# A two-layer hybrid decoder trunk on one core: v and probabilities copied by ScalarE, and another split of the first phase's side work

## The chip, the cores and the metric

The kernel runs on one core of one Trainium2 chip. The metric is the device time of one execution in microseconds. Engine names in the rows: PE is TensorE, PEld its weight loads, DVE is VectorE, ACT is ScalarE, POOL is GpSimd, SP is the engine that issues the DMAs.

## The reference

512 tokens of width 1024 go through two layers; each layer is a feed-forward half step, a token mixer and a second feed-forward half step, all in float32. Cut to what matters:

```python
for l in range(2):
    mod = (silu(c) @ w_ada[l] + b_ada[l]).reshape(b, 9, d)
    h = rmsnorm(x, norm_g[l, 0]) * (1 + mod[:, 1]) + mod[:, 0]
    x = x + 0.5 * mod[:, 2] * swiglu(h, w_ffn_in[l, 0], w_ffn_out[l, 0])
    h = rmsnorm(x, norm_g[l, 1]) * (1 + mod[:, 4]) + mod[:, 3]
    x = x + mod[:, 5] * token_mixer(h, l, ...)
    h = rmsnorm(x, norm_g[l, 2]) * (1 + mod[:, 7]) + mod[:, 6]
    x = x + 0.5 * mod[:, 8] * swiglu(h, w_ffn_in[l, 1], w_ffn_out[l, 1])

def token_mixer(h):                       # three branches, gated and summed
    qa, ka, va, qb, kb, vb, u = split(h @ w_in)
    # A: 8 heads of 64, three dilated windows, combined by their denominators
    # B: 4 heads, difference of two softmaxes: p0 / sum(p0) - lam * p1 / sum(p1)
    # C: GLU, causal depthwise convolution of 31 taps, layer norm, swish
    y = sum_i sigmoid(h @ w_gate_i) * (branch_i @ w_branch_i)
    return y @ w_out
```

## The kernel before

**Products.** Activations lie with the 1024 features on partitions, as 8 chunks of 128 x 512 tokens. Each float32 operand is held as a high and a low half, and each product is three TensorE matmuls: high by high, high by low, low by high (`mm_steps`; the rows show them as L274, L276 and L278). For a weight tile, `halves` makes the high half `wh` by a ScalarE copy (L226) and the low half `wl` by a subtraction (L230), on VectorE mostly, and on GpSimd for the weights of the first phase (`kind == "first"`) and a few others (`second`). Weights come by DMA on SP's queue into 5 raw tiles; `load` issues the DMA and the two halves, and `weight` keeps two weights loaded ahead (`AHEAD`) before it hands one out.

**Six stages.** Feed-forward 1 takes the time to about 355 us, mixer 1 to 956, the other two feed-forwards of the middle to 1644, mixer 2 to 2217 and the last feed-forward the rest. In feed-forward 1 the first phase works on the fly: for each chunk k, `first(k)` normalizes chunk k (`norm_h`: `hx` on VectorE, L491; `hh`, its high half, on ScalarE, L493; `hl`, its low half, on VectorE, L500), and TensorE then does 18 products of 512 columns with chunk k and the weight `("first", k)` into six PSUM banks. Between `hx` and `hl` stands `modulation(k + 1)`: it makes the modulation vectors of the next chunk. `ada` (L430, L431) loads a 128 x 1024 weight and multiplies and sums it with the broadcast `cb`; `ada_done` adds the bias and makes the 128x1 columns `amp` (L444, L445) and `shift` (L442), all on VectorE. After the phase stand a plain block (m = 3) and pairs of blocks by Strassen-like products (`pair`, L583), whose seven weights come in the order p = 1, 2, 6, 7, 5, 3, 4 from four raw tiles (`block`, L242 to L254). `more(k)` between the blocks puts k further `ada` jobs, the modulation vectors that later stages need, behind each.

**Attention.** In the mixer, `project` makes q, k and v of a pair of A heads or of one B head: PSUM to `qk` by ScalarE (L841), to the high half of v by VectorE (L842) and to its low half by VectorE (L843). `scores` does six products of 64 rows (three for each half of the partitions, L896) into two PSUM banks of the tag `s`, VectorE adds the bias and takes the maximum (L903, `m`), ScalarE the exponential (L905), VectorE the reciprocal of the denominator (L921). `sa` then scales the probabilities by it on VectorE: both halves in an A head (L925), one of them in a B head (L928). `sb` transposes the probabilities on TensorE (L938) into a bank of `s` and splits them into halves (`pT`, L268 and L269); `pv` and `sc` multiply them with v (L965, L980, L983). These steps of one head and the projection of the next are woven into each other by generators (`pull`), and the convolution's taps (L770, VectorE, 240 in all) are put among them by a rhythm.

**What sets the order.** A tile scheduler lays down each engine's static order from its own estimates; semaphores then make an engine wait at run time. In `setup` and `first`, `manual_schedule` keeps VectorE in program order. PSUM has 4 banks of the tag `mm`, 3 of `s` and 1 of `o`; `whi` and `wlo` have 3 tiles each.

Of the kernel before, what the change touches and what calls it, by code (L numbers as in the profile page):

```python
# [16 lines left out]
AF = mybir.ActivationFunctionType  # L17
# [5 lines left out]
D = 1024  # L23
# [50 lines left out]
class Trunk:  # L74
# [146 lines left out]
    def halves(self, key, raw, n):  # L221
        nc = self.nc
        kind = key[0]
        hi = self.wp.tile([P, 1024], F32R, tag="whi", name=self.name("wh"), bufs=3)
        lo = self.wp.tile([P, 1024], F32R, tag="wlo", name=self.name("wl"), bufs=3)
        nc.scalar.activation(hi[:, :n], raw[:, :n], AF.Copy)  # L226

        second = (kind == "u" and key[2] == 0) or (kind == "in" and key[3:] == (0, 1))
        eng = nc.gpsimd if kind == "first" or second else nc.vector
        eng.tensor_tensor(lo[:, :n], raw[:, :n], hi[:, :n].bitcast(F32), op=ALU.subtract)  # L230
        return hi, lo

# [102 lines left out]
    def setup(self):  # L335
        nc, io, cp = self.nc, self.io, self.cp
        self.par = cp.tile([P, L, NPAR], F32, name="par")
        row = self.t4k([P, D], F32, "crow")
        nc.scalar.dma_start(row[0:1, :], io["c"])
        nc.scalar.dma_start(self.par[:, 0, :], io["par"][:, 0, :])  # L340
        xt = cp.tile([P, KD, T], F32, name="x")
        self.x = [xt[:, k, :] for k in range(KD)]
        for k in range(0, KD, 2):
            nc.sync.dma_start(xt[:, k:k + 2, :], io["x"][:, k:k + 2, :])
        self.h = [(cp.tile([P, T], F32R, name=f"hh{k}"), cp.tile([P, T], F32R, name=f"hl{k}"))
                  for k in range(KD)]
        self.acc = cp.tile([P, T], F32, name="ssq")
        self.sq7 = cp.tile([P, T], F32, name="sq7")
        self.ident = cp.tile([P, P], F32, name="ident")
        make_identity(nc, self.ident)  # L350
        self.ones = cp.tile([P, 2], F32, name="ones")
        nc.vector.memset(self.ones, 1.0)
        self.mod = [cp.tile([P, 72], F32, name=f"mod{l}") for l in range(L)]
        self.shift = [cp.tile([P, 24], F32, name=f"shift{l}") for l in range(L)]
        self.amp = [cp.tile([P, 24], F32, name=f"amp{l}") for l in range(L)]
        self.res = [cp.tile([P, 24], F32, name=f"res{l}") for l in range(L)]
        nc.scalar.activation(row[0:1, :], row[0:1, :], AF.Silu)
        cb = self.t4k([P, D], F32, "cb")
        for a in range(0, D, T):
            ps = self.bank("mm")  # L360
            nc.tensor.matmul(ps, self.ones[0:1, 0:1].to_broadcast([1, P]), row[0:1, a:a + T],
                             start=True, stop=True)
            nc.scalar.activation(cb[:, a:a + T], ps, AF.Copy)
        for k in range(KD):
            sq = self.t2k("sq") if k > 1 else (self.acc, self.sq7)[k]
            nc.scalar.activation(sq, self.x[k], AF.Square)
            if k > 1:
                a = (self.acc, self.sq7)[k % 2]
                nc.vector.tensor_tensor(a, a, sq, op=ALU.add)
        nc.vector.tensor_tensor(self.acc, self.acc, self.sq7, op=ALU.add)  # L370
        self.ada(cb, 0, 8)
        v = self.token_sum([self.acc], range(4), 1.0 / D, EPS)
        return cb, self.token_bcast(self.rsqrt(v, 4), range(4))

    def p(self, l, o, n=1):
        return self.par[:, l, o:o + n]
# [269 lines left out]
    def ffn(self, n, l, f, ada, cb, stats, nxt, first=None):  # L646
        nc, io = self.nc, self.io
        s = 2 * f
        acts = {}

        def finish(m, pg, pu):
            sl = self.t2k("sil")
            nc.scalar.activation(sl, pg, AF.Silu)
            nc.vector.tensor_tensor(sl, sl, pu, op=ALU.mult)
            acts[m] = self.act_pair("a")
            self.split(acts[m], sl)

        def unit(g):
            return lambda d: self.weight("down", l, f, g, d)

        def more(k):
            for _ in range(k):
                if ada:
                    ada.popleft()(cb)

        if first:
            banks = [self.bank(t) for t in ("mm", "mm", "mm", "mm", "s", "s")]
            for k in range(KD):
                w = first(k)
                for j in range(6):  # L670
                    self.mm(banks[j], w, slice(j * P, (j + 1) * P), self.h[k], k == 0, k == KD - 1)
            for m in range(3):
                finish(m, banks[2 * m], banks[2 * m + 1])
            self.sums()
            self.ready = True
        early = []
        blocks = self.ffn_blocks(n)
        st = {}
        for (kind, i), after in zip(blocks, blocks[1:] + [("end", 0)]):
            if kind == "plain":  # L680
                if i == 0:
                    early = self.head(lambda j: self.weight("in", l, f, j // 2, j % 2))
                    self.sums()
                ps = []
                for j in range(2):
                    if early:
                        ps.append(early.pop(0))
                        continue
                    w = self.weight("in", l, f, i, j)
                    ps.append(self.bank("mm"))  # L690
                    self.mmk(ps[j], w, self.h, range(KD), 0, KD - 1)
                finish(i, ps[0], ps[1])
                if first:
                    more(4)
            elif kind == "pair":
                down = (lambda g=after[1]: self.down(l, f, g, 0, acts)) if after[0] == "down" else None
                st = self.pair(l, f, i, st, after[1] if after[0] == "pair" else None, acts, down)
                if first or i > 2:
                    more(2 if first else 1)
            else:  # L700
                more(2)
                for d in range(1, KD):
                    self.down(l, f, i, d, acts)
                    more(2)
        more(len(ada or ()))
        self.tail(l, s, unit(2), acts, GROUPS[2], GROUPS[2][0], stats, nxt)
# [110 lines left out]
    def project(self, l, i, st):  # L817
# [3 lines left out]
        for sub in range(4):  # L821
# [4 lines left out]
            for t in range(4):  # L826
                for kk in range(2):
                    k = sub * 2 + kk
                    hs = slice(t * P, (t + 1) * P)
                    ws = slice(kk * 384, (kk + 1) * 384)  # L830
                    hi, lo = self.h[k]
                    o = ps[t][:, 0:384]
                    nc.tensor.matmul(o, hi[:, hs], w[0][:, ws], start=k == 0, stop=False)  # L833
                    yield
                    nc.tensor.matmul(o, hi[:, hs], w[1][:, ws], start=False, stop=False)  # L835
                    yield
                    nc.tensor.matmul(o, lo[:, hs], w[0][:, ws], start=False, stop=k == KD - 1)  # L837
                    if k < KD - 1:
                        yield
                if sub == 3:  # L840
                    nc.scalar.activation(qk[:, t, :], ps[t][:, 0:256], AF.Copy)  # L841
                    nc.vector.tensor_copy(v[:, 0, t, :], ps[t][:, 256:384])  # L842
                    nc.vector.tensor_tensor(v[:, 1, t, :], ps[t][:, 256:384],  # L843
                                            v[:, 0, t, :].bitcast(F32), op=ALU.subtract)
                    if t == 3:
                        self.qk_norm(l, i, st)
                    yield
# [61 lines left out]
    def attention(self, l, i, st, ys, pull, before):  # L909
# [6 lines left out]
        def sa(n):  # L916
# [5 lines left out]
            if A:  # L922
                dat[n] = [e0, e1]
                for j, e in enumerate(dat[n]):
                    nc.vector.tensor_scalar(e[:, 0:w], e[:, 0:w], rd[:, j:j + 1], None, op0=ALU.mult)  # L925
                return
            nc.vector.tensor_tensor(rd[:, 1:2], rd[:, 1:2], self.neglam[:, l:l + 1], op=ALU.mult)
            nc.vector.tensor_scalar(e1[:, 0:w], e1[:, 0:w], rd[:, 1:2], None, op0=ALU.mult)  # L928
            nc.vector.scalar_tensor_tensor(e0[:, 0:w], e0[:, 0:w], rd[:, 0:1], e1[:, 0:w],
                                           op0=ALU.mult, op1=ALU.add)  # L930
            dat[n] = [e0]
# [196 lines left out]
    def run(self, stop=6):  # L1128
        nc, io = self.nc, self.io

        def modulation(k):
            if k < KD:
                if k:
                    self.ada(cb, 0, 8 + k)
                self.ada(cb, 0, k)
                self.ada_done(0, 0, 1, (k, k + 1))
                self.ada_done(0, 0, 0, (k, k + 1))

        def first(k):
            with self.tc.manual_schedule(engines={mybir.EngineType.DVE}):  # L1140
                self.norm_h(0, 0, k, pb, FULL, lambda: modulation(k + 1))
            return self.weight("first", k)

        with self.tc.manual_schedule(engines={mybir.EngineType.DVE}):
            cb, pb = self.setup()
# [100 lines left out]
```

## Time and profile before

| | us |
|---|---|
| Median of 3 runs | 2555.83 (2554.1 to 2555.9) |
| The profiled execution | 2555.3 |
| Its span in the profile | 2553.2 |
| PE busy | 2486.7 (97%) |
| DVE busy | 1965.9 (77%) |
| ACT busy | 1123.4 (44%) |
| POOL busy | 30.6 (1%) |
| Mean granted clock of TensorE | 0.992 |

The span counts from the first to the last recorded instruction; 2.1 us of the execution lie outside of it. TensorE's clock has two levels, and 1.00 in the rows is 2.4 GHz. A matmul's busy time overlaps with that of the next, so the distance between two starts tells more than the duration. Rows of the timeline put several like instructions into one (x2, x6); an entry in brackets is the idle time ahead of it and what ended it.

### The profile page before, as it was taken

The page shows a single profiled execution, that of the slowest core. Times are in us where ns is not written, and L with a number is a line of the kernel's source. Part 1 is how long each engine was busy: PE and PEld are TensorE (multiplying, and loading weights), DVE is VectorE, ACT ScalarE, POOL GpSimd, SP SyncE. Part 2 cuts the span into 40 slices and gives each one's busy share as a digit, 9 for nine tenths or more (in the row PEclk, how much of TensorE's full clock was granted, in tenths as well). Part 3 has the DMA queues.
Part 4 walks back from the last instruction along what each step waited for, and adds up shares of the span by engine and source line. Part 5 has one row for each costly group of instructions (what it writes and reads, how often), then busy time and mean ns, then how long its engine had stood idle before and what let it go on. Part 6 is the DMA issues. An engine that isn't in the chain of part 4 may idle for free.

```text
span 2553.2 us, 37958 instructions
## 1 busy us (share of the span) xinstructions
PE 2486.7 (97%) x15072; PEld 2192.3 (86%) x15072; DVE 1965.9 (77%) x3519; ACT 1123.4 (44%) x1765; POOL 30.6 (1%) x33
## 2 busy tenths in 40 slices
PE   6899999999999999999989999999999999999999
PEld 5889898888778889898989898888787788898988
DVE  8998876999965478979678886679999554885855
ACT  4435343554553355343455252435555433552523
POOL 2000000000000000000000000000000000000000
PEclk9999999999999999999999999999999999999999
DMA  7564744312223323737324554332122233233332
GB/s 268 165 248 149 247 146 127 91 57 75 79 83 108 91 75 101 263 101 263 108 67 143 213 167 148 99 87 75 54 84 75 75 115 91 65 103 99 109 97 85
DMA packets 97747, 312.20 MB, mean 122 GB/s; under 512 B 10345, under 2 KB 17257, under 8 KB 97570
## 3 DMA queue, kind: packets, MB, share of 16 engines
q1 hardware_dynamic: 97424, 309.65, 38.1%
q8 instruction: 118, 1.93, 0.3%
q14 instruction: 59, 0.48, 0.1%
q10 hardware_dynamic: 146, 0.14, 0.0%
HBM read 307.62 MB, written 6.06 MB: 123 GB/s over the span
## 4 chain that ended last, share of the span: by engine, by line
PE 81%; DVE 12%; ACT 3%; DMA 2%; issue 2%; POOL 0%; DVEq 0%; SPq 0%; ACTq 0%
PE mm L583 15%; PE mm L274 14%; PE mm L276 14%; PE mm L278 14%; PE s L583 11%; PE mm L837 3%; PE mm L835 3%; PE mm L833 3%; DVE wl L230 2%; PE s L896 2%; DVE wr L770 1%; DMA wr<-in_w_up 1%; PE o L965 1%; PE s L938 1%; DVE ada L431 1%
## 5 line engine op out<-in xcount | busy, mean ns | idle before, releaser
L226 ACT ACTIVATE wh<-wr 128x1024 fp32r<-128x1024 f32 (+1 forms) x481 | 485.3, 1010 | 623.8 <-PE mm L278 299.0
L230 DVE TENSOR_TENSOR wl<-wr,wh 128x1024 fp32r<-128x1024 f32 (+1 forms) x468 | 544.3, 1165 | 206.3 <-ACT wh L226 205.1
L274 PE MATMUL mm<-ah,wh 128*128 128x512 f32 (+1 forms) x752 | 287.2, 383 | 0.0
L278 PE MATMUL mm<-al,wh 128*128 128x512 f32 (+1 forms) x752 | 286.7, 382 | 0.0
L276 PE MATMUL mm<-hh,wl 128*128 128x512 f32 (+1 forms) x776 | 281.5, 366 | 5.2 <-DVE wl L230 5.2
L276 PE MATMUL mm<-ah,wl 128*128 128x512 f32 (+1 forms) x752 | 286.3, 382 | 0.0
L274 PE MATMUL mm<-hh,wh 128*128 128x512 f32 (+1 forms) x776 | 281.5, 366 | 5.0 <-ACT hh L493 2.7
L583 PE MATMUL mm<-sh,wh 128*128 128x256 f32 x936 | 268.8, 287 | 16.9 <-ACT wh L226 14.1
L278 PE MATMUL mm<-hl,wh 128*128 128x512 f32 (+1 forms) x776 | 276.2, 367 | 5.8 <-DVE hl L500 5.6
L583 PE MATMUL mm<-sh,wl 128*128 128x256 f32 x936 | 268.4, 287 | 0.5 <-DVE wl L230 0.5
L583 PE MATMUL mm<-sl,wh 128*128 128x256 f32 x936 | 268.1, 286 | 0.0
L509 DVE SCALAR_TENSOR_TENSOR x<-mm,res,x 128x512 f32<-128x512 f32 (+1 forms) x124 | 86.1, 697 | 156.5 <-PE mm L278 156.5
L583 PEld LDWEIGHTS mm<-sh,wh 128*128 128x128 f32 x936 | 182.5, 195 | 18.9 <-ACT wh L226 14.9
L583 PEld LDWEIGHTS mm<-sh,wl 128*128 128x128 f32 x936 | 182.9, 195 | 1.2 <-DVE wl L230 0.8
L583 PEld LDWEIGHTS mm<-sl,wh 128*128 128x128 f32 x936 | 183.0, 196 | 0.0
L835 PE MATMUL mm<-wl,hh 128*128 128x384 f32 x512 | 179.7, 351 | 1.3 <-DVE wl L230 1.2
L837 PE MATMUL mm<-wh,hl 128*128 128x384 f32 x512 | 180.6, 353 | 0.0
L431 DVE SCALAR_TENSOR_TENSOR ada<-ada,cb 128x1024 f32<-128x1024 f32 x144 | 174.2, 1225 | 4.2 <-DMA ada<-in_w_ada 4.0
L833 PE MATMUL mm<-wh,hh 128*128 128x384 f32 x512 | 175.3, 347 | 1.8 <-DVE v L843 1.8
L770 DVE SCALAR_TENSOR_TENSOR wr<-u,par,wr 128x512 f32<-128x512 f32 x240 | 175.9, 744 | 0.5
L583 PE MATMUL s<-hh,wl 128*128 128x256 f32 x624 | 174.1, 279 | 1.2 <-DVE wl L230 1.2
L583 PE MATMUL s<-hl,wh 128*128 128x256 f32 x624 | 175.1, 281 | 0.0
(214 smaller groups left out, 5551.1 us busy)
## 6 DMA issues: line engine op xcount, KB each, us to landing
wr<-in_w_up SPq DMA_DIRECT2D x156, 512.0 KB, 3.7
ada<-in_w_ada SPq DMA_DIRECT2D x144, 512.0 KB, 5.7
wr<-in_w_down SPq DMA_DIRECT2D x64, 512.0 KB, 4.8
wr<-in_w_qkv SPq DMA_DIRECT2D x64, 384.0 KB, 3.2
wr<-in_w_gate SPq DMA_DIRECT2D x48, 512.0 KB, 3.7
wr<-in_w_down SPq DMA_DIRECT2D x32, 384.0 KB, 3.1
wr<-in_w_branch SPq DMA_DIRECT2D x24, 512.0 KB, 3.6
wr<-in_w_u SPq DMA_DIRECT2D x16, 512.0 KB, 3.6
```

What stands on the lines that cost most here:

```text
L226: nc.scalar.activation(hi[:, :n], raw[:, :n], AF.Copy)
L230: eng.tensor_tensor(lo[:, :n], raw[:, :n], hi[:, :n].bitcast(F32), op=ALU.subtract)
L274: nc.tensor.matmul(ps[:, rng], w[0][:, wcol], ah[:, rng], start=start, stop=False)
L276: nc.tensor.matmul(ps[:, rng], w[1][:, wcol], ah[:, rng], start=False, stop=False)
L278: nc.tensor.matmul(ps[:, rng], w[0][:, wcol], al[:, rng], start=False, stop=stop)
L431: nc.vector.scalar_tensor_tensor(w, w, 1.0, cb, op0=ALU.mult, op1=ALU.mult, accum_out=self.mod[l][:, e:e + 1])
L509: self.nc.vector.scalar_tensor_tensor(self.x[d][:, rng], ps[:, rng], self.res[l][:, 8 * s + d:8 * s + d + 1], self.x[d][:, rng], op0=ALU.m ...
L583: nc.tensor.matmul(o, w[a][:, c], acts[k][b], start=first and (mi, k, x) == (0, 0, 0), stop=(k, x) == (3, 2), skip_group_check=True)
L770: nc.vector.scalar_tensor_tensor(ca[j], u, w, ca[j], op0=ALU.mult, op1=ALU.add)
L833: nc.tensor.matmul(o, hi[:, hs], w[0][:, ws], start=k == 0, stop=False)
L835: nc.tensor.matmul(o, hi[:, hs], w[1][:, ws], start=False, stop=False)
L837: nc.tensor.matmul(o, lo[:, hs], w[0][:, ws], start=False, stop=k == KD - 1)
```

## The change

Five edits. (1) `halves`: the low halves of the eight weights of the first phase go from GpSimd to VectorE, and `first` takes its weight inside the manual order. (2) `setup`: the first two weights are loaded ahead of the sum over tokens, and the sum that `ada(cb, 0, 8)` makes comes after the reciprocal root. (3) `modulation`: `amp` and `shift` of a chunk are made by ScalarE, two activations of 128x1, from a column `nb` = (bias + 1) * norm that is made once; before, VectorE used three operations for them. (4) feed-forward 1's `more`: four `ada` jobs are no longer behind the plain block, and pairs 2 and 3 have three and five instead of two each; the total is the same. (5) attention: 64 copies of v's high half (L842) and 96 scalings of probabilities (L925, 64 of them, and L928, 32) go from VectorE to ScalarE.

```diff
 def halves(self, key, raw, n):
...
-        eng = nc.gpsimd if kind == "first" or second else nc.vector
+        eng = nc.gpsimd if second else nc.vector
 def setup(self):
...
+        while len(self.loaded) < AHEAD:
+            self.load()
+        v = self.token_sum([self.acc], range(4), 1.0 / D, EPS)
+        pb = self.token_bcast(self.rsqrt(v, 4), range(4))
         self.ada(cb, 0, 8)
-        v = self.token_sum([self.acc], range(4), 1.0 / D, EPS)
-        return cb, self.token_bcast(self.rsqrt(v, 4), range(4))
+
+        nb = self.small(8, "nb")
+        nc.vector.scalar_tensor_tensor(nb, self.p(0, PO_BADA + 8, 8), 1.0, self.p(0, PO_NORM, 8),
+                                       op0=ALU.add, op1=ALU.mult)
+        self.nb = nb
+        return cb, pb
...
-                if first:
-                    more(4)
...
-                    more(2 if first else 1)
+                    more({2: 3, 3: 5}.get(i, 2) if first else 1)
 def project(self, l, i, st):
...
-                    nc.vector.tensor_copy(v[:, 0, t, :], ps[t][:, 256:384])
+                    nc.scalar.activation(v[:, 0, t, :], ps[t][:, 256:384], AF.Copy)
 def attention(self, l, i, st, ys, pull, before):
...
-                    nc.vector.tensor_scalar(e[:, 0:w], e[:, 0:w], rd[:, j:j + 1], None, op0=ALU.mult)
+                    nc.scalar.activation(e[:, 0:w], e[:, 0:w], AF.Copy, scale=rd[:, j:j + 1])
...
-            nc.vector.tensor_scalar(e1[:, 0:w], e1[:, 0:w], rd[:, 1:2], None, op0=ALU.mult)
+            nc.scalar.activation(e1[:, 0:w], e1[:, 0:w], AF.Copy, scale=rd[:, 1:2])
...
         def modulation(k):
...
-                self.ada_done(0, 0, 1, (k, k + 1))
-                self.ada_done(0, 0, 0, (k, k + 1))
+                c = slice(k, k + 1)
+                nc.scalar.activation(self.amp[0][:, c], self.mod[0][:, 8 + k:9 + k], AF.Identity,
+                                     scale=self.p(0, PO_NORM + k), bias=self.nb[:, c])
+                nc.scalar.activation(self.shift[0][:, c], self.mod[0][:, c], AF.Identity,
+                                     bias=self.p(0, PO_BADA + k))
         def first(k):
             with self.tc.manual_schedule(engines={mybir.EngineType.DVE}):
                 self.norm_h(0, 0, k, pb, FULL, lambda: modulation(k + 1))
-            return self.weight("first", k)
+                return self.weight("first", k)
```

Beside the code, the scheduler lays the engines' rows down anew. TensorE has the same instructions; its order differs in the first 97 us and in the attention of each layer (1357 rows each), and nowhere else. At three places the orders stand as follows; line numbers behind the change are those of the changed file.

On VectorE, one cycle of the first phase, before; `hx` and `hl` belong to a chunk, the `ada` rows to the next chunk's modulation:

```order
L491 SCALAR_TENSOR_TENSOR hx_282<-x,amp_111,s_169 128x512
L431 SCALAR_TENSOR_TENSOR ada_287,mod_107<-ada_287,cb_116 128x1024
L431 SCALAR_TENSOR_TENSOR ada_290,mod_107<-ada_290,cb_116 128x1024
L444 TENSOR_TENSOR mod_107<-mod_107,par 128x1
L445 SCALAR_TENSOR_TENSOR amp_111<-mod_107,par 128x1
L442 TENSOR_TENSOR shift_109<-mod_107,par 128x1
L500 SCALAR_TENSOR_TENSOR hl_87<-hx_282,shift_109,hh_86 128x512
L491 SCALAR_TENSOR_TENSOR hx_324<-x,amp_111,s_169 128x512
```

The same cycle on VectorE after:

```order
L500 SCALAR_TENSOR_TENSOR hx_281<-x,amp_111,s_178 128x512
L440 SCALAR_TENSOR_TENSOR ada_286,mod_107<-ada_286,cb_116 128x1024
L440 SCALAR_TENSOR_TENSOR ada_289,mod_107<-ada_289,cb_116 128x1024
L509 SCALAR_TENSOR_TENSOR hl_87<-hx_281,shift_109,hh_86 128x512
L230 TENSOR_TENSOR wl_298<-wr_295,wh_297 128x768
L500 SCALAR_TENSOR_TENSOR hx_322<-x,amp_111,s_178 128x512
```

The three 128x1 operations are gone from VectorE, and the low half of a weight stands behind `hl`.

On VectorE, later in feed-forward 1, from the low half of the third weight of pair 4 (p = 6, made from the tile `t`) to that of the fourth (p = 7), before:

```order
L230 TENSOR_TENSOR wl_1162<-t_1159,wh_1161 128x1024
L630 TENSOR_TENSOR u_151_980<-u_151_980,s_982 128x512
L431 SCALAR_TENSOR_TENSOR ada_1382,mod_107<-ada_1382,cb_116 128x1024
L632 TENSOR_TENSOR act_1136<-u_151_980,c_161_1047 128x2x256
L230 TENSOR_TENSOR wl_1192<-wr_1015,wh_1191 128x1024
```

And after:

```order
L230 TENSOR_TENSOR wl_1156<-t_1153,wh_1155 128x1024
L269 TENSOR_TENSOR al_1128<-act_1121,ah_1127 128x1024
L250 TENSOR_TENSOR wr_1000<-wr_1002,wr_1000 128x1024
L253 TENSOR_TENSOR wr_998<-wr_998,t_1153 128x1024
L440 SCALAR_TENSOR_TENSOR ada_1376,mod_107<-ada_1376,cb_116 128x1024
L230 TENSOR_TENSOR wl_1186<-wr_1000,wh_1185 128x1024
```

Between the two low halves now stand four operations of 1024 columns, where one of them and two smaller ones stood; the others were further ahead in the order before.

On TensorE, the last score step (four blocks of keys, 128x512) of the first head pair in layer 1, before; `s_4669` and `s_4670` are the banks of the two halves, the `mm` rows are the next projection and the `o` rows products with v:

```order
L837 MATMUL mm_4600<-wh_4605,hl_89 128x384
L833 MATMUL mm_4601<-wh_4605,hh_86 128x384
L896 MATMUL s_4669<-qT_4469,qT_4458 128x512 x2
L896 MATMUL s_4670<-qT_4469,qT_4458 128x512 x2
L896 MATMUL s_4669<-qT_4469,qT_4458 128x512
L896 MATMUL s_4670<-qT_4469,qT_4458 128x512
L965 MATMUL o_4691<-pT_4595,v_4269 128x512 x2
```

And after:

```order
L904 MATMUL s_4663<-qT_4463,qT_4452 128x512 x3
L843 MATMUL mm_4594<-wl_4600,hh_88 128x384
L845 MATMUL mm_4594<-wh_4599,hl_89 128x384
L841 MATMUL mm_4595<-wh_4599,hh_86 128x384
L843 MATMUL mm_4595<-wl_4600,hh_86 128x384
L973 MATMUL o_4685<-pT_4589,v_4263 128x512
L904 MATMUL s_4664<-qT_4463,qT_4452 128x512 x3
```

The six score products stood together; now the three of one half and the three of the other have five products of 128 rows between them.

## Rows read from the trace of the kernel before

**Rows 1.** The page, part 4: shares of the chain of work that ended last:

```profile
PE 81%; DVE 12%; ACT 3%; DMA 2%; issue 2%; POOL 0%; DVEq 0%; SPq 0%; ACTq 0%
```

**Rows 2.** Windows: us, length, busy us (instructions) by engine, PEclk, DMA, GB/s:

```profile
520.00:560.00 40.00, 39.95 (x235) 34.49 (x234) 37.47 (x111) 22.93 (x62) 0.00 (x0) 1.00 0.17 46
...
840.00:880.00 40.00, 40.00 (x173) 32.00 (x173) 16.16 (x19) 9.93 (x13) 0.00 (x0) 1.00 0.31 92
440.00:720.00 280.00, 275.07 (x1495) 231.17 (x1493) 264.40 (x751) 145.11 (x338) 0.00 (x0) 0.99 0.25 73
```

**Rows 3.** Timeline, first phase: start us, us, engine line op out<-in xcount [idle <-releaser]:

```profile
12.11 4.64 POOL L230 TENSOR_TENSOR wl<-wr,wh 128x768 fp32r<-128x768 f32 x2 [1.07 <-ACT wh L226]
...
15.21 1.57 DVE L295 TENSOR_SCALAR rs<-ts 128x4 int32<-128x4 int32 x1
16.81 0.17 DVE L296 TENSOR_SCALAR rs<-rs 128x4 int32<-128x4 int32 x1
...
20.98 0.75 DVE L491 SCALAR_TENSOR_TENSOR hx<-x,amp,s 128x512 f32<-128x512 f32 x1 [0.75 <-PE s L331]
...
24.12 1.80 DVE L445 SCALAR_TENSOR_TENSOR amp<-mod,par 128x1 f32<-128x1 f32 x1
```

**Rows 4.** Timeline of DVE, first phase, the end of one cycle and the next:

```profile
48.70 1.22 DVE L431 SCALAR_TENSOR_TENSOR ada<-ada,cb 128x1024 f32<-128x1024 f32 x1
...
51.84 0.74 DVE L500 SCALAR_TENSOR_TENSOR hl<-hx,shift,hh 128x512 fp32r<-128x512 f32 x1
52.51 0.73 DVE L491 SCALAR_TENSOR_TENSOR hx<-x,amp,s 128x512 f32<-128x512 f32 x1
...
58.12 0.74 DVE L491 SCALAR_TENSOR_TENSOR hx<-x,amp,s 128x512 f32<-128x512 f32 x1
```

**Rows 5.** Timeline of PE and DVE, feed-forward 1, pairs:

```profile
87.97 0.58 PE L583 MATMUL mm<-sh,wh 128*128 128x256 f32 x1 [6.06 <-ACT wh L226]
...
128.26 1.22 DVE L230 TENSOR_TENSOR wl<-t,wh 128x1024 fp32r<-128x1024 f32 x1
...
134.40 0.28 PE L583 MATMUL s<-sh,wl 128*128 128x256 f32 x1
```

**Rows 6.** Groups of instructions: xcount | busy us, mean ns | idle us, releasers:

```profile
L230 DVE TENSOR_TENSOR wl<-wr,wh 128x768 fp32r<-128x768 f32 x96 | 91.0, 951 | 14.3 <-ACT wh L226 13.9
...
L842 DVE CAST v<-mm 128x128 fp32r<-128x128 f32 x64 | 17.3, 284 | 2.5 <-ACT qk L841 2.2
...
L925 DVE TENSOR_SCALAR p<-p,rd 128x128 f32<-128x128 f32 (+3 forms) x64 | 22.4, 379 | 0.1
...
L905 ACT ACTIVATE p<-p,m 128x128 f32<-128x128 f32 (+3 forms) x128 | 71.0, 556 | 44.4 <-DVE m L903 34.9 <-DVE rt L311 7.3 <-DVE ss L859 1.4
```

**Rows 7.** Timeline of PE, score steps of 512 columns in three forms:

```profile
581.35 0.97 PE L896 MATMUL s<-qT,qT 64*128 64x512 f32 x3
...
644.77 0.50 PE L896 MATMUL s<-qT,qT 64*128 64x512 f32 x2
...
645.57 0.50 PE L896 MATMUL s<-qT,qT 64*128 64x512 f32 x2
...
686.69 0.98 PE L896 MATMUL s<-qT,qT 64*128 64x512 f32 x6
687.59 0.50 PE L276 MATMUL mm<-yh,wl 128*128 128x512 f32 x1
```

**Rows 8.** Timeline of PE, a stretch of waits in layer 1:

```profile
572.69 0.33 PE L938 MATMUL s<-ident,p 128*128 128x128 f32 x1 [0.51 <-DVE m L903]
...
573.93 0.85 PE L896 MATMUL s<-qT,qT 64*128 64x384 f32 x3 [0.91 <-DVE m L903]
...
576.67 0.69 PE L835 MATMUL mm<-wl,hh 128*128 128x384 f32 x1 [0.33 <-DVE wl L230]
```

**Rows 9.** Windows, stretches at half clock, columns as in rows 2:

```profile
574.60:581.30 6.70, 6.13 (x19) 4.86 (x18) 5.31 (x21) 1.47 (x5) 0.00 (x0) 0.50 0.23 59
...
1840.90:1844.20 3.30, 3.30 (x11) 2.72 (x10) 2.25 (x8) 1.88 (x6) 0.00 (x0) 0.50 0.37 112
```

## The prediction

> **What bounds the kernel now.** First the shares of the chain that ended last: TensorE has 81% of it, VectorE 12% [rows 1]. So the time is TensorE's own work plus the places where it waits, and there mostly for VectorE. Next the windows [rows 2]: in the branch products (840 to 880 us) 173 matmuls of 512 columns take 40 us, 0.231 us each, and VectorE is busy 16 of 40 us; nothing that frees VectorE can help there. In attention (440 to 720 us) VectorE is busy 264 of 280 us, in 520 to 560 even 37.5 of 40, ScalarE only 145 of 280. TensorE shows as busy there too, but it takes more than its pitch for many instructions. Third the timeline of the first phase [rows 3, 4], where VectorE's own chain sets the pace. In the other feed-forwards and in what follows attention the orders are unchanged, and I take their time as unchanged.
>
> **First phase.** A cycle from hx to hx takes 5.61 us (52.51 to 58.12) [rows 4]. Before the first chunk, while GpSimd's pair of subtractions runs (12.11 to 16.75), a 128x4 operation of VectorE at 15.21 takes 1.57 us; its twin at 16.81, right behind the pair, takes 0.17 [rows 3]. In the cycles the amp operation of 128x1, which starts with GpSimd's subtraction of the next weight, takes 1.80 us (24.12) [rows 3]. So the GpSimd work costs VectorE about 1.63 us in a cycle, though no semaphore is between them. After the change a cycle on VectorE holds hx, two sums of 1.14, hl, and one low half. The durations are 0.73, 1.22, 1.22, 0.74 and 0.95 us [rows 4, 6]; successive starts come some 0.08 earlier than the durations say (51.84 to 52.51 is 0.67 for a row of 0.74), so the cycle is 0.66 + 2.28 + 0.67 + 0.87 = 4.48 us. amp and shift go to ScalarE, which has room: they need the sums only, and hl and a low half lie between the sums and the next hx, 1.5 us of cover against two small activations. If that cover fails, hx waits. hx of the first chunk, at 20.98 now [rows 3], comes about 1.5 earlier by the root operation, near 19.4; the first cycle has no low half, since two weights are loaded ahead, so the last hx comes at 19.4 + 3.6 + 6 x 4.48 = 49.9 to 50.5, instead of 58.12 [rows 4]: 8 us earlier. TensorE's need per chunk, 18 x 0.231 = 4.16 us, stays under the cycle.
>
> **How much of these 8 us survives.** VectorE remains the pace-setter for a while: the ada jobs and the low halves up to pair 4 are the same in number. TensorE's wait of 6.06 us at 87.97 [rows 5], with a half-clock stretch around it (0.50 from 86.5 to 93.2) in the trace, shrinks or goes, but that is not the last one. I stepped VectorE's new order with the durations above. In pair 4 the order now puts four operations of 1024 columns between two low halves that TensorE needs one after the other. The first of the two ends near 120.5 and TensorE, by its own work, would ask for it near 117.5; the second is asked for again too early, and TensorE takes it up near 126.2. Before, the same product starts at 134.40, its low half's operation having begun at 128.26 with no wait left [rows 5]. The gain is 134.4 - 126.2 = 8.2. I take off about 1 for ada's DMA behind a buffer of tag z. **Term: -7.** Ends: -13, if these two waits of 3 us each do not come, and -1, if ScalarE's amp or weight copies are late and the cycle becomes 5.4 us.
>
> **Attention, engine work.** VectorE loses 64 x 0.284 = 18 us (L842) and 96 x 0.379 = 36 us (L925; L928's 32 have the same shapes) [rows 6], together 54 us or 27 per layer of its 264. ScalarE gains 96 activations; the nearest row is the exponential on the same tiles, 0.556 us [rows 6], so 53 us, and 64 copies of 128 columns, which by the same row are under 36 us: at most 44 per layer on top of 145, 189 of 280. None of it is on TensorE's path where its cover holds: a scaled probability is wanted by a transpose only one score step later.
>
> **Attention, TensorE's order.** This speaks against the change. A score product uses 64 rows, and the trace shows what it costs to go between those and the 128-row products [rows 7]. Six in a row take 0.90 us to the next start (686.69 to 687.59). In pairs with one filler between, a pair and a filler take 0.80 (644.77 to 645.57); less the filler's 0.17 a pair costs 0.63, three of them 1.89. And three of one half alone take 0.97 us, as much as all six of both halves together (0.98): the two halves no longer run side by side. So a step of 512 columns costs 1.0 us over its fillers as one block, 1.8 to 1.9 in pairs, and 2 x 0.97 and the slow filler behind each, 2.1 to 2.3, in split halves. Counting the new order against the old, in each layer three steps of 512 columns go from one block to split halves (+1.05 to +1.25 each), three steps from one block to pairs (+0.75 each), two others change by +0.3 and -0.7: 5.3 us per layer. **Term: +10.5**, ends 8 and 12.
>
> A rule bears on this. The Trainium skill, "TensorEngine Tiling (Array Packing)", Key Properties, says that a change of the tiling mode drains TensorE, and that tiles work in parallel. By the number of changes alone (268 become 312 over both layers, at an estimated 0.2 us from the difference of pairs and block, 0.8 / 4) the term would be 8.8 and the sum 2546; the row of three at 0.97 shows the second half of the rule as well, and I keep 10.5.
>
> **Attention, waits.** The largest stall is from 572.69 to 576.67: four waits, the first 0.51, then 0.91 for the maximum of a score bank, the last 0.33 for a low half [rows 8]; with the stretched instructions about 3 us are lost. It is VectorE's backlog: its reductions, taps, scalings and v copies come in between. Behind it the clock is at 0.50 for 6.7 us [rows 9], which costs about 3.35. The same cluster stands in layer 2, again about 3, with 3.3 us at 0.50 [rows 9], some 1.65. Together 11 us. In the new order VectorE's work ahead of the stall loses two v copies and four scalings, 2 x 0.284 + 4 x 0.379 = 2.1 us by their means [rows 6], 1.6 by their shapes there; that is more than any single wait of the four, and TensorE does not get there earlier, so the cluster goes and the clock with it. TensorE's other idle time in 440 to 720 is 280 - 275.07 = 4.9 [rows 2] less the cluster's 2, 3 us per layer in small waits, partly for ScalarE; I take them as unchanged, since what VectorE gives back there, ScalarE's queue may take. **Term: -11.** Ends: -17, when these 2 x 3 go too, and +3, when the cluster stays and ScalarE adds one of its size.
>
> **Sum.** The profiled execution took 2555.3, 0.5 under the median, which is inside the spread of the runs. 2555.3 - 7 + 10.5 - 11 = 2547.8: **2548**. With the terms' nearer ends, 2541 to 2551.
>
> **Rivals.** *The order's price is paid, the waits stay.* 2555.3 - 7 + 10.5 - 0 to 2 = 2556.5 to 2559: no change. For it: TensorE is 81% of the chain and VectorE 12%, so freeing VectorE buys little, and the cost in the order is certain. Against it: VectorE's 264 of 280. *Both gains are larger.* Pair 4's waits don't come and nearly all waits in attention go: 2555.3 - 13 + 10.5 - 17 = 2536. *The first phase gives little,* since amp comes late behind ScalarE's weight copies: 2555.3 - 1.5 + 10.5 - 11 = 2553. *Slower:* in the B heads the scaling now crosses from VectorE (reciprocal, times lambda) to ScalarE and back to VectorE, where all stood in a row on one engine. If that chain comes later than TensorE's transposes, each of the 32 B steps costs about 0.3 to 0.4 us, the extent of a scaling of 0.379: 10 to 13 us, and the cluster's gain is lost too: 2555.3 - 7 + 10.5 + 9 = 2568. It decides once the scaled probabilities arrive behind the transposes' turn; for it speaks the exponential's queue on ScalarE, against it that a whole score step lies between.
>
> **Chances.** Forecast 0.45; both gains larger 0.15; waits stay 0.22; first phase gives little 0.05; slower 0.13. A measurement of this kernel can tell about 0.2%, 5.1 us, from no change. Under 2550.7 counts as faster: 0.45 + 0.15 = 0.60. Within: 0.22 + 0.05 = 0.27. Slower: 0.13. The range is 2538 to 2562: it leaves out about half of the better case and nearly all of the slower one, 0.2 together, and takes in the ends of the terms and the case of no change.
>
> **What the profile after would show.** Right: no 1.8 us operations of 128x1 on VectorE; hx every 4.5 us, the last near 50; the product that stood at 134.40 near 127; score steps of layer 1 in split halves at 2.2 us; no half clock near 574 and 1840. Wrong: hx starts that wait for ScalarE's amp; a new half-clock stretch in feed-forward 1, where TensorE waits for pair 4's low halves; TensorE's transposes waiting for `p` from ScalarE; VectorE still full in 520 to 560 because it waits rather than works.

## The result, and the profile after

| | before | after |
|---|---|---|
| Median, us | 2555.62 (2554.1 to 2555.9, 4 runs) | 2522.00 (2520.5 to 2522.3, 4 runs) |
| Profiled execution | 2555.3 | 2520.5 |
| PE busy | 2486.7 (97%) | 2470.0 (98%) |
| DVE busy | 1965.9 | 1924.0 |
| ACT busy | 1123.4 | 1179.6 |

The ratio is 0.9868 (0.9856 to 0.9881): 33.6 us faster. All times here are medians of runs that agree within 0.3%; one run of v alone (4914.2 us) and one with the weights moved (3312.8 us) took far longer and are left out. The sign was forecast, the size was not: 2548 and a range down to 2538, so the time lies 26 us under the forecast and 16 under the range.

The page of the changed kernel, its chain, which answers to [rows 1]:

```profile
PE 86%; DVE 9%; ACT 3%; issue 2%; DMA 1%; SPq 0%; DVEq 0%; ACTq 0%
```

VectorE's share of the chain fell from 12 to 9%. The timeline of VectorE in the first phase after, the end of one cycle and the next, answers to [rows 4]:

```profile
45.03 0.73 DVE L500 SCALAR_TENSOR_TENSOR hx<-x,amp,s 128x512 f32<-128x512 f32 x1
45.69 1.21 DVE L440 SCALAR_TENSOR_TENSOR ada<-ada,cb 128x1024 f32<-128x1024 f32 x1
...
46.84 1.22 DVE L440 SCALAR_TENSOR_TENSOR ada<-ada,cb 128x1024 f32<-128x1024 f32 x1
...
47.98 0.74 DVE L509 SCALAR_TENSOR_TENSOR hl<-hx,shift,hh 128x512 fp32r<-128x512 f32 x1
48.65 0.94 DVE L230 TENSOR_TENSOR wl<-wr,wh 128x768 fp32r<-128x768 f32 x1
49.52 0.73 DVE L500 SCALAR_TENSOR_TENSOR hx<-x,amp,s 128x512 f32<-128x512 f32 x1
```

The cycle is 4.49 us, the last hx at 49.52: the prediction had 4.48 and 49.9 to 50.5. In attention, what TensorE waited for in layer 1 (engine, line, releaser: us in total, times, longest), first before, from 443 to 723.6, then after, from 430 to 706.4:

```profile
PE mm L274 <- ACT wh L226: 1.1, 1, 1.1
PE s L896 <- DVE m L903: 0.9, 1, 0.9
PE mm L833 <- DVE v L843: 0.9, 1, 0.9
PE s L938 <- DVE m L903: 0.5, 1, 0.5
...
```

```profile
PE mm L274 <- ACT wh L226: 0.9, 1, 0.9
PE s L1019 <- DVE y L1012: 0.4, 1, 0.4
```

The cluster of [rows 8] is gone, and with it the half clock of [rows 9]. But none of these accounts for what the windows show where nothing was changed, in the down products of feed-forward 1, before and after (columns as in rows 2):

```profile
155.00:185.00 30.00, 30.00 (x130) 24.12 (x129) 26.74 (x38) 6.35 (x6) 0.00 (x0) 1.00 0.75 261
```

```profile
145.00:175.00 30.00, 30.00 (x133) 24.62 (x132) 26.79 (x39) 6.60 (x7) 0.00 (x0) 1.00 0.72 254
```

TensorE is busy without a pause at full clock in both, the products are the same, and 133 of them fit where 130 did. Matched one by one, a product of 512 columns from ah, al or the y and z tiles takes mostly 226 to 232 ns to the next start, and took 231 to 238.

### The profile page after: what moved, and what is told of

Read it like the earlier page. It is cut to its first block, busy times and chain, and to the rows that moved or that the text cites. A ratio compares the mean times of both kernels' runs of the same rounds, so it can differ in the third digit from the quotient of the medians.

```text
span 2518.7 us, 37996 instructions
## 1 busy us (share of the span) xinstructions
PE 2470.0 (98%) x15072; PEld 2186.7 (87%) x15072; DVE 1924.0 (76%) x3344; ACT 1179.6 (47%) x1941; POOL 15.3 (1%) x25
## 4 chain that ended last, share of the span: by engine, by line
PE 86%; DVE 9%; ACT 3%; issue 2%; DMA 1%; SPq 0%; DVEq 0%; ACTq 0%
PE mm L592 16%; PE mm L274 14%; PE mm L276 14%; PE mm L278 14%; PE s L592 12%; PE mm L845 3%; PE mm L843 3%; PE mm L841 3%; PE s L904 2%; DVE wl L230 2%; PE o L973 1%; PE s L946 1%; DVE wr L778 1%; ACT wh L226 1%; ACT hh L502 1%
## 5 line engine op out<-in xcount | busy, mean ns | idle before, releaser
L230 DVE TENSOR_TENSOR wl<-wr,wh 128x1024 fp32r<-128x1024 f32 (+1 forms) x476 | 551.6, 1161 | 215.7 <-ACT wh L226 214.5
L843 PE MATMUL mm<-wl,hh 128*128 128x384 f32 x512 | 179.5, 351 | 0.0
L592 PE MATMUL s<-hh,wh 128*128 128x256 f32 x624 | 174.8, 280 | 0.0
```

The lines of the kernel that those rows point to most:

```text
L592: nc.tensor.matmul(o, w[a][:, c], acts[k][b], start=first and (mi, k, x) == (0, 0, 0), stop=(k, x) == (3, 2), skip_group_check=True)
```

## The experiments

The one thing that differs there is where the tiles lie. `nb` is the first column tile of eight in its pool and is made ahead of z, ah and al; these start 160 bytes per partition further on (five buffers of 32 bytes). Addresses are those of the built programs; the traces hold none. So the first runs take the change apart by addresses, first phase and attention.

**Addresses alone**, with the order of before on every engine:

```diff
+        nb = self.small(8, "nb")
+        nc.vector.memset(nb, 0.0)
         self.ada(cb, 0, 8)
         v = self.token_sum([self.acc], range(4), 1.0 / D, EPS)
```

> The kernel before with one unused column tile of 128x8 made (and cleared) in setup, which is where the changed kernel makes nb. Every engine keeps the order of before; only the addresses of the tiles behind it move by 160 bytes per partition, those of ah, al, yh, yl, zh, zl and z among them, as in the changed kernel. Theory A (part of the gain is the new addresses): the changed trace shows products with 512 columns of ah, al, yh, yl, zh and zl at 226 to 232 ns to the next start where before shows 231 to 238, about 4.9 ns less for each of 2256 products, 11 us: 2544.5 us. Theory B (the shorter pitch comes from less VectorE work, or is a matter of the chip): 2555.6 us, no change.

Measured: 2540.7 us (0.9949, 0.9934 to 0.9964), 14 us gained by a column that nobody reads. Its window in the same products:

```profile
155.00:185.00 30.00, 30.00 (x133) 24.63 (x132) 27.23 (x39) 6.37 (x6) 0.00 (x0) 1.00 0.77 268
```

133 again. The expectation counted too few products: with the y and z tiles there are 944 of 512 columns in each of the three kinds, 2832; times 5 ns that is 14 us.

**The changed kernel with the addresses of before:**

```diff
-        nb = self.small(8, "nb")
+        nb = self.res[1][:, 0:8]
```

> The changed kernel with nb kept in columns of res that are not used yet, so that no tile's address differs from before; every engine keeps the changed order. Theory A: 11 us above the changed kernel, 2533 us. Theory B: as the changed kernel, 2522 us.

Measured: 2537.7 us (0.9934, 0.9919 to 0.9949), 15.7 above the changed kernel, and 130 products in the window:

```profile
145.00:175.00 30.00, 30.00 (x130) 24.13 (x129) 27.69 (x41) 6.31 (x7) 0.00 (x0) 1.00 0.77 268
```

Theory B falls in both directions. What the change meant to do is worth the rest, 17 to 19 us.

**First phase and rhythm alone** (the changed kernel without edit 5, addresses of before).

> The change's first phase and rhythm of ada jobs (edits 1 to 4) with the addresses of before, and attention as before. The two traces put the last product of the first feed-forward's pairs 12.3 us earlier (356.4 to 344.1), of which by theory A some 1.7 us are addresses: 10.6 us, 2545 us. By the prediction's term it would be 7 us, 2548.6; if the gain shown there is given back later, under 5.

Measured: 2543.6 us (0.9959, 0.9944 to 0.9974), 11.4 us gained. TensorE's waits in pair 4:

```profile
116.62 0.39 PE L592 MATMUL mm<-sh,wh 128*128 128x256 f32 x1 [1.03 <-ACT wh L226]
...
117.88 0.39 PE L592 MATMUL mm<-sh,wl 128*128 128x256 f32 x1 [0.87 <-DVE wl L230]
...
124.02 0.39 PE L592 MATMUL mm<-sh,wh 128*128 128x256 f32 x1 [1.52 <-ACT wh L226]
124.25 0.28 PE L592 MATMUL s<-sh,wl 128*128 128x256 f32 x1
```

Ahead of them the same products start 16.0 us earlier than before; behind them 10.3 us: the stall that the prediction saw in the order stands where it was foreseen and takes 5.7 us back. Half clock is part of it, from 118.3 to 121.7. Its first product was foreseen near 120.5 and the second near 126.2; they are at 117.9 and 124.25. The order of TensorE differs here too, beside the places named with the change: the product at 124.02, of the next weight, stood 23 places further back before, and now the second one stands behind its wait for ScalarE.

**Attention alone** (edit 5 on the kernel before).

> The kernel before with edit 5 alone (v and probabilities by ScalarE), the addresses of before. The traces put the stretch from the first product of the projection to the last score product 4.3 us (layer 1) and 3.9 us (layer 2) shorter, up to 1 us of each by theory A from addresses: 6 to 8 us in all, 2548 to 2549 us. By the prediction's terms (10.5 lost in the order, 11 gained in waits) no change, 2555.

Measured: 2547.0 us (0.9970, 0.9960 to 0.9980), 7.9 us gained. The three parts, addresses, first phase and attention, add up to 14.2 + 11.4 + 7.9 = 33.5 of 33.6.

**v alone, probabilities alone.**

> The kernel before with the 64 copies of v's high half on ScalarE, probabilities as before, addresses of before. Its score steps cost some 2 us less than those of before. Theory D: 17 us leave VectorE, half of what the other part takes off, so the cluster of waits is eased but may not go: 4 to 8 us gained with the order, 2547 to 2551 us. Rival (only the scalings, which stand right in the chain of a score step, matter): 2553.

> The kernel before with the 96 scalings of probabilities on ScalarE, v as before, addresses of before. In its order the score steps cost some 7 us more than in that of before, by the costs that the attention run shows for each form. Theory D (VectorE's backlog in attention sets TensorE's waits; 36 us leave VectorE): the waits give 10 to 13 us, 2549 to 2552 us. Rival (the scalings now come late for the transposes): 2560 or more.

Measured: v alone 2538.7 us (0.9934, 0.9915 to 0.9954), probabilities alone 2543.1 (0.9952, 0.9937 to 0.9967); both gain more than was expected. v alone gains clearly more than both together; for the probabilities the intervals overlap, and the windows put them 0.8 us per layer ahead of both. The windows of layer 1 from the first product of the projection to the last score step, in the order before, both edits, v alone, probabilities alone:

```profile
443.00:723.60 280.60, 275.67 (x1499) 230.99 (x1498) 263.33 (x753) 147.84 (x342) 0.00 (x0) 0.99 0.25 73
```

```profile
442.20:718.70 276.50, 275.29 (x1501) 229.70 (x1499) 246.72 (x675) 172.98 (x420) 0.00 (x0) 1.00 0.25 74
```

```profile
442.80:716.10 273.30, 270.93 (x1500) 227.53 (x1498) 257.64 (x721) 153.26 (x374) 0.00 (x0) 1.00 0.25 75
```

```profile
444.70:720.40 275.70, 274.80 (x1500) 229.47 (x1499) 252.35 (x707) 168.40 (x388) 0.00 (x0) 1.00 0.25 74
```

Each holds the same work. TensorE's idle time (length less PE busy) is 4.9, 1.2, 2.4 and 0.9 us, and only the first window still has half clock, 6.8 us of it: either edit takes most of the waits away, so the second has little left to give. What the order costs is worked out from the starts in each trace. A score step counts from its first product to the product behind its last, less the other products in between at their usual pitch (0.174 us for 384 columns, 0.231 for 512). The 32 steps of layer 1 take 39.2, 41.4, 35.6 and 41.0 us. Before, 2.0 us of that are the stall of [rows 8], in the step at 573.93, and 0.9 the wait for v (L843) in the list above, which falls inside a step of 256 columns; with v alone 0.4 are waits. Without them the steps take 36.2, 41.4, 35.2 and 41.0 us. So edit 5's order costs 5.1 us per layer over before, and v alone's saves 1.0. The window of both edits is 4.1 us shorter than before all the same, so some 9.2 us of waits have gone from layer 1. One step of 512 columns, first in the changed kernel and then with v alone:

```profile
562.78 0.96 PE L904 MATMUL s<-qT,qT 64*128 64x512 f32 x3
563.66 0.44 PE L845 MATMUL mm<-wh,hl 128*128 128x384 f32 x1
...
565.56 0.96 PE L904 MATMUL s<-qT,qT 64*128 64x512 f32 x3
```

```profile
575.67 0.96 PE L896 MATMUL s<-qT,qT 64*128 64x512 f32 x6
576.57 1.08 PE L965 MATMUL o<-pT,v 128*128 128x512 f32 x4
```

Twice 0.96 us for three products against once for six, as in [rows 7]. Counted as above, the four such steps of the changed layer 1 take 1.97 to 1.99 us each, a step in pairs 1.7, and one in a block 0.9 to 1.06.

**Which edit of the first phase.** Three runs, with attention and addresses of before: edits 1, 2 and 4 without amp and shift on ScalarE; edits 2 to 4 with the low halves left on GpSimd; edits 1 to 3 with the old rhythm.

> Edits 1, 2 and 4 without edit 3: the low halves of the first phase's weights by VectorE, amp and shift by VectorE as before; attention and addresses as before. Theory P (GpSimd's subtraction holds VectorE's small operation for 1.6 us a cycle): the cycle is 4.48 us and three operations of some 0.15, 4.9 to 5.0 us, the last hx some 3 us later than with edit 3; what of it survives pair 4 is the same 3 us: 2546 to 2547 us, where all four edits gave 2543.6. Rival (amp and shift on ScalarE are what counts): no gain, 2555.

> Edits 2 to 4 without edit 1: amp and shift by ScalarE, the low halves of the first phase's weights by GpSimd as before; attention and addresses as before. Theory P (GpSimd's subtraction holds whatever VectorE starts beside it): GpSimd's 1.8 us now hold hl or hx of a cycle, which stays at 5.1 us or more, and little is left: 2550 to 2555 us. Rival (what was held was the 128x1 operations alone, so without them nothing is): as all four edits, 2543.

> Edits 1 to 3 without edit 4: the ada jobs again four behind the plain block and two behind each pair. The number up to pair 4 is the same, so VectorE arrives at pair 4's low halves at the same time and TensorE waits there up to the same point; only the early lead of 16 us differs. By the stepping of the prediction: 2543 to 2545 us, as with edit 4. Rival (the rhythm makes part of the gain): 2547 or more.

Measured: 2543.4 us (0.9955, 0.9940 to 0.9970), 2545.0 (0.9960, 0.9945 to 0.9974) and 2547.3 (0.9968, 0.9957 to 0.9980). The first beats its expectation by 3 us and cannot be told from all four edits, though its cycle is 4.82 us instead of 4.48: its lead is 14.8 us ahead of pair 4, where theirs is 16.0, and 8.1 behind it, where theirs is 10.3. Nearly all of the phase's gain is there without edit 3. With GpSimd out of the way the amp operation, 1.80 us in [rows 3], takes 0.16:

```profile
45.66 0.16 DVE L454 SCALAR_TENSOR_TENSOR amp<-mod,par 128x1 f32<-128x1 f32 x1
```

The second misses its expectation and lies near the rival's 2543. With GpSimd still at work the cycle is 4.62 us:

```profile
36.55 0.74 DVE L509 SCALAR_TENSOR_TENSOR hl<-hx,shift,hh 128x512 fp32r<-128x512 f32 x1
...
36.72 2.29 POOL L230 TENSOR_TENSOR wl<-wr,wh 128x768 fp32r<-128x768 f32 x1 [2.32 <-ACT wh L226]
...
37.21 0.74 DVE L500 SCALAR_TENSOR_TENSOR hx<-x,amp,s 128x512 f32<-128x512 f32 x1
...
37.87 2.22 DVE L440 SCALAR_TENSOR_TENSOR ada<-ada,cb 128x1024 f32<-128x1024 f32 x1
```

hl had begun ahead of GpSimd and hx runs beside it at its usual 0.74; only the sum is held, 2.22 instead of 1.22 us. So GpSimd does hold VectorE, but 1.0 us of its time and not 1.6, since hx, one of whose two tiles lies in PSUM, goes through. By the Trainium skill, "SBUF — State Buffer", Who interferes with whom, a VectorE instruction with two SBUF inputs and a GpSimd instruction that reads SBUF exclude each other, whoever is first, and one with a single SBUF input is free outside the modes that use both ports: these rows agree. The 128x4 operation of [rows 3] reads a single tile and was held nonetheless, which is not explained here. The third run goes as its rival had it and shows what edit 4 is worth, 3.7 us: without it the wait comes at once behind the phase (6.81 us at 79.8, with half clock) and the lead stays at 8.0 through the rest of feed-forward 1. No run has edits 2 and 4 alone, so what they give without both of the others is not shown.

**How addresses act.** Four runs, each with the order of its base: z, ah and al moved by 32 or by 64 bytes instead of 160; the weight tiles moved by 32 (and not alone, as the expectation says: sh, sl, ah and al behind them moved by 64, hh and hl stayed); and the changed kernel with hh and hl moved by 32 (the tiles behind them by 64).

> The kernel before with an unused column of 32 bytes ahead of z, ah and al, order of before: these tiles start at 32 instead of 0 within 64 bytes, 128 bytes away from where the layout run put them. Theory A1 and A2 (relation of the moving tile to the weight tile, which starts at 32): as the layout run, 2541 us. Theory A3 (some other distance counts): anything else.

> The same with 64 bytes: z, ah and al stay at 0 within 64 bytes, at new addresses. Theory A1 and A2: no change, 2555 us. Theory A3: a gain.

> The kernel before with only the weight tiles (raw, high and low half) moved by 32 bytes, so that they start at 0 within 64 bytes like ah, al, hh and hl. Theory A1 (the moving tile alone): products of 512 columns from ah and hh stay at 234 ns, 2555 us; the projections, where the weights are the moving side, would get slower. Theory A2 (moving and stationary tile at equal places are fast): the products from ah, al, hh and hl all get shorter, 14 + 8 us, 2533 us.

> The changed kernel with a column of 32 bytes ahead of the tiles hh and hl and one behind them: hh and hl start at 32 instead of 0 within 64 bytes, all other large tiles stay as in the changed kernel, and so does every order. Theory A1 (what counts is where within 64 bytes the moving tile starts): the 1608 products of 512 columns from hh and hl get 4.9 ns shorter, 8 us, 2514 us. Theory A3 (it is a matter of these tiles' pool or of what else uses them): no change, 2522.

Measured: 2551.0 us (0.9983, 0.9974 to 0.9993), 2551.8 (0.9987, 0.9978 to 0.9997), 2545.8 (0.9963, 0.9949 to 0.9977) and 2528.4, 6.4 above the changed kernel. None is as theory A1 or A2 had it. By matched products: with the weights moved, 512 columns from hh and hl fall from 233.2 to 228.0 ns though neither tile moved, and 256 columns from them rise from 117.5 to 119.8, while 256 columns from sh and sl fall from 119.9 to 117.8. So it is not the moving tile's address alone; moving the weights changes what products from hh and hl cost. With hh and hl moved, their 512 columns fall to 228 as well, but their 3528 products of 256 columns rise to 119.8, and ah's of 512 columns rise from 229 to 232.8 though ah lies at the same distance from the weights, counted within 512 bytes. So equal distance is not the whole rule either.

A prediction could be made of it all the same. Products of 256 columns took 119.8 to 120.0 ns wherever moving and weight tile start at the same place within 256 bytes, and less elsewhere. In the kernel before and in the changed one, sh, sl and the weights start at 160 within 256, hh and hl at 192. The next run moves sh and sl to 192:

```diff
+        pt4 = self.ap_.tile([P, 8], F32, tag="pt4", name="pt4", bufs=1)
+        nc.vector.memset(pt4, 0.0)
         row = self.t4k([P, D], F32, "crow")
...
-        return self.ap_.tile([P, n], dt, tag=f"small{n}", name=self.name(s), bufs=5)
+        return self.ap_.tile([P, n], dt, tag=f"small{n}", name=self.name(s), bufs=4 if n == 8 else 5)
```

> The changed kernel with the tiles sh and sl (and the others of their pool tag, down to hx) moved by 32 bytes; ah, al, hh, hl and the weights stay, and so does every order. In the runs so far the 256-column products of a moving tile and a weight tile whose start addresses are equal within 256 bytes take 119.8 ns, and 116 to 118.5 where they are not: sh and sl stand at an equal place with the weights, hh and hl stood there only where they or the weights were moved. Theory A2 (relation of moving and weight tile): 2808 products get some 2 ns shorter, 5 to 6 us, 2516 us. Theory A1 (the moving tile alone): no change or either sign, 2522.

Measured: 2512.6 us (0.9832, 0.9818 to 0.9847), 9.4 under the changed kernel. In the windows of a pair's products, the changed kernel and this one:

```profile
190.00:220.00 30.00, 30.00 (x254) 30.00 (x253) 26.94 (x30) 15.57 (x19) 0.00 (x0) 1.00 0.49 159
```

```profile
190.00:220.00 30.00, 30.00 (x259) 30.00 (x259) 26.82 (x30) 16.09 (x19) 0.00 (x0) 1.00 0.53 177
```

259 products instead of 254, 2.3 ns less for each. Matched one by one, the 3744 products from sh and sl (the expectation counted 2808) fall by 3.1 ns, 12 us. The 2808 from hh and hl fall as well, by 0.6 to 1.1 ns, though neither they nor the weights moved, so the rule foresaw where the gain lies but does not explain all of it. Part is lost again at half clock, which takes 19.8 us of this profile and 13.0 of the changed kernel's (length times the share of clock not granted).

**The best of both:** the last kernel with the probabilities back on VectorE.

```diff
-                    nc.scalar.activation(e[:, 0:w], e[:, 0:w], AF.Copy, scale=rd[:, j:j + 1])
+                    nc.vector.tensor_scalar(e[:, 0:w], e[:, 0:w], rd[:, j:j + 1], None, op0=ALU.mult)
...
-            nc.scalar.activation(e1[:, 0:w], e1[:, 0:w], AF.Copy, scale=rd[:, 1:2])
+            nc.vector.tensor_scalar(e1[:, 0:w], e1[:, 0:w], rd[:, 1:2], None, op0=ALU.mult)
```

> The first phase's edits, v by ScalarE, the probabilities back on VectorE, and the addresses of the run with sh and sl moved. Attention's order is that of v alone. Theory S (both attention edits free VectorE enough, but the order that the scheduler makes of both together costs 5 to 6 us more per layer in score steps than that of v alone, while the waits it saves beyond v alone are some 1 to 2 us): 2512.6 - 6.5 = 2506 us. Rival (v alone's gain was of its addresses or its stretch only, and does not add to the rest): 2512 or more.

Measured: 2506.6 us (0.9808, 0.9792 to 0.9825), 15.4 us under the changed kernel and 49 under the one before. Theory S holds in size: by the steps above the order of both costs 6.1 us more per layer than that of v alone, and the waits that both save beyond v alone are 2.9.

## Why the prediction was wrong

- **"I take their time as unchanged", of the stages whose orders don't change.** This is the step that failed: it put at nothing, because the order stays, what the run with addresses alone measures at 14.2 us, of the 26 that the forecast was off. The order was unchanged there, the addresses were not, and nothing in the prediction's views tells of addresses. The pitch in [rows 2] was carried over as it was; it goes with the layout.
- **First phase, -7; measured -11.4.** The mechanism was right: cycle, place of the last hx, and the stall in pair 4 that takes part of it back. Mis-sized was the stepping up to pair 4, 2 to 3 us late (126.2 against 124.25), and the 1 us taken off for ada's DMA did not show. One of its signs of being wrong did come: half clock in feed-forward 1 at pair 4's low halves, from 122.5 to 125.9 us in the changed kernel. GpSimd's hold was right for the operations that were there; that amp and shift alone would nearly do was not seen.
- **The order of score steps, +10.5; worked out from the starts, +10.2** (twice 5.1). This term was right, step by step: a step of 512 columns in split halves costs 0.9 to 1.1 us more than in a block, where 1.05 to 1.25 was used, and one in pairs 0.8 more, where 0.75 was used. By the number of changes alone, the rule of the Trainium skill ("TensorEngine Tiling (Array Packing)", Key Properties) had given 8.8; the row of three at 0.97 was rightly kept beside it. v alone shows the same: it leaves seven of the eight steps of 512 columns in layer 1 whole, before it is six, with both edits two.
- **Waits in attention, -11; by difference -18.1** (7.9 gained in all, and 10.2 paid for the order). The cluster and its half clock went, as foreseen. Mis-sized by 7 us was the rest: the small waits "taken as unchanged" went too, TensorE's idle time falls from 4.9 to 1.2 us in layer 1. The prediction's far end was -17. Idle time and half clock together make up 7.1 of the 9.2 us in layer 1; where the other 2 lie is open.
- **The rivals.** "Both gains are larger" (2536) is nearest: without the new addresses the changed kernel takes 2537.7. Of its two conditions one held: nearly all waits in attention went, but pair 4's came. "The waits stay" (its sum comes to 2556.8 to 2558.8) and "slower" did not come: no transpose waits for a scaled probability.

## To carry to other kernels

Before a gain in unchanged code is explained, count instructions per window there: more of the same in the same busy time is a different pitch, and a new tile, however small, can be its cause. When one of two edits already empties the waits, the second only costs what its order costs; try each alone. A lead won at the start is worth what is left of it behind the next place where the same engine is late.

## What the runs showed of the hardware

A matmul's pitch at full clock depends on where its operands lie: 226 to 238 ns for 512 columns and 115 to 120 for 256. Before, 512 columns from ah take 234.2 to 234.3 ns in the mean of every stage; 160 bytes further on they take 228.3 to 228.9. The Trainium skill, "TensorE: Matmul & The Clock Gate", Wait — 56ns, not 53.3ns?, gives the columns at 2.4 GHz and about 2.5 ns, 215.7 for 512; no run here comes that low. What in the addresses decides stays open: the start of the moving tile alone and the distance to the weight tile were tried and do not explain all rows. The half-clock stretches at the seams between stages come and go with the version; with those in feed-forward 1 and attention they take 12 to 26 us in sum, so that a few us between two versions can be that.
